# Differential attention: VectorE does all of the mix of the two softmaxes, GpSimd none

## The chip, the cores and the metric

The kernel runs on one core of a Trainium2 chip. The metric is the device time of one execution in microseconds (us), the median of the runs shown. One more execution was recorded by the hardware profiler; its page and its trace are what the prediction reads. Engines go by short names: PE (matmul; PEld is its weight load), DVE (VectorE), ACT (ScalarE), POOL (GpSimd), SP (the engine that issues most DMAs).

## The reference, cut to what matters

Two transformer layers over 2048 tokens of width 1024, float32. The first layer has three kinds of attention side by side; the change touches one, differential attention with six heads. Each head has two components with 32 features each; the weights of the second softmax, times lambda, are taken from those of the first, and the difference is multiplied with the values:

```python
s = jnp.einsum('bqhcd,bkhcd->bhcqk', qi, k) * scale
causal = key_idx[None, :] <= q_idx[:, None]
p = jax.nn.softmax(jnp.where(causal, s, NEG_BIG), axis=-1)
a = p[:, :, 0] - lam * p[:, :, 1]
return jnp.einsum('bhqk,bkhd->bqhd', a, v)
```

Afterwards comes an rms norm over the 64 features of each head. Since that norm takes out any factor common to a row, the kernel does not divide by the first softmax's sum s0. It forms exp0 + c * exp1 with c = -lambda * s0 / s1, one number for each row.

## The kernel before, in words

`differential` (line 599) handles 24 units in order: three pairs of heads p, two halves k, four steps j. A unit is two blocks of 128 queries, a high one and a low one, chosen so that their causal keys are 17 blocks of 128 together. The low block has nlo = 4k + j + 1 blocks of keys (1 to 8), the high one 17 - nlo (16 to 9). For each of the two heads and each of the two components a unit has one tile `row` of 2176 columns: first the high block's columns, then, from column n on, the low block's.

Three stages run one unit apart. While unit s + 2 has its scores computed, unit s + 1 is mixed and unit s is multiplied with the values.

- Scores (`diff_scores`): PE multiplies queries and keys into one of three PSUM banks `psz` (the tag "z": 3 in line 1386). DVE moves each chunk of up to 512 columns from there into `row`, times a scale, and keeps its smallest element in `mn` (line 725; line 727 where the causal mask applies; line 731 joins minima). ACT then takes the exponentials in place and sums them.
- Mix (`diff_mix`, line 748): DVE inverts the second sums (line 762) and forms the two factors c, one for each block of queries, in a tile `tiny` of 128x2 (line 766). Then exp0 + c * exp1 is formed over the 17 blocks. With a = 128 * max(0, 5 - nlo), GpSimd takes columns a to n in two instructions, a product in place (line 771) and a sum (line 772). DVE takes the low block's columns, n to 2176, in pieces of up to 1024, and columns 0 to a, each in one fused multiply-add `scalar_tensor_tensor` (line 778). So DVE takes max(5, nlo) of the 17 blocks, GpSimd the other 9 to 12.
- Values (`diff_values`): PE transposes blocks of `row` into PSUM (`pstp`), ACT copies them out (`wT`), PE multiplies with the values (`pspv`); after a chunk of queries comes the norm (`diff_norm`).

Between them go steps of `filler` (line 866), a share of the output projection: ACT and GpSimd split activations `mp` in two parts (line 901 is GpSimd's), PE multiplies them (`psmm`), DVE adds the residual (line 912). DVE itself splits five weight tiles `wo` (line 881).

PE's and ACT's instructions stay in the order in which the code writes them. DVE's, GpSimd's and SP's are put in an order by a scheduler when the kernel is built, and each engine works through its own in that order. In each unit the steps of scores and mix are spread over four beats; `diff_mix` returns its steps by beat, and the lists are mixed evenly with the work of the values and the filler.

Of the kernel before, what the change touches and what calls it, by code (L numbers as in the profile page):

```python
# [15 lines left out]
S = 2048  # L16
D = 1024
P = 128
# [16 lines left out]
VBLOCKS = 5  # L35
MIX = 1024
# [9 lines left out]
class Pinned:  # L46
    """An engine whose instructions stay in the order in which they are written."""
# [18 lines left out]
class Net:  # L66
# [16 lines left out]
    def phase(self, bufs, banks, side="left"):  # L83
        """Pools for one phase; SBUF slots and PSUM banks by tag."""
# [29 lines left out]
    def turn(self, key, pattern):  # L114
        """The next letter of a repeated pattern: which engine takes this one."""
        k = self.turns.get(key, 0)
        self.turns[key] = k + 1
        return pattern[k % len(pattern)]
# [8 lines left out]
    def consts(self):  # L127
# [5 lines left out]
        # nothing, then what is after the query (a column further on: at it or after it)  # L133
# [12 lines left out]
        # -lambda on every partition  # L146
# [26 lines left out]
    def rope_tables(self, k, sink):  # L173
        """cos and sin of the positions' angles, in chunks of 512: sink(chunk, cos, sin)."""
        nc = self.nc
        for t in range(NT):
# [5 lines left out]
            n = self.t("c2")  # L182
# [10 lines left out]
    def wtile(self, src):  # L193
        """A [P, 8, 128] tile of weights, as two parts."""
        w, (fill,) = self.wtile_steps(src, 1, self.nc.gpsimd)
        fill()
        return w
# [21 lines left out]
    def load_x(self, between):  # L219
        """x transposed, [tc][half] -> (hi, lo) of [P, 4, 512]."""  # L220
        nc = self.nc
        self.xs = []
        for t in range(NT):
            row = []
# [18 lines left out]
    def proj_t(self, w, t):  # L243
        """[128 features, 512 tokens] of chunk t."""
        return self.proj_side([w], t)[0]

    def proj_side(self, ws, t):
        """The same for several tiles of weights side by side."""
# [8 lines left out]
    def spill_parts(self, ps, dst, t, scale=None):  # L257
        """ps (times a power of two) in two parts to dst [2, P, S]."""
# [112 lines left out]
    def rope_all(self):  # L371
        """Both layers' tables to DRAM, a chunk of one at each next()."""
# [13 lines left out]
    def vtile(self, g):  # L386
        """Weights of 256 columns of the two attentions' values, as two parts of each half."""
# [9 lines left out]
    def values(self, g, ws, side):  # L397
        """256 columns of the two attentions' values, token by token."""
# [19 lines left out]
    def dup_parts(self, hi, lo, src, hh):  # L418
        """Half hh of src's partitions, its two parts in both halves of hi and lo."""
# [13 lines left out]
    def memkv(self, W, mem, keep):  # L433
        """Memory keys of each pair of heads and all values, a weight tile at each next()."""
# [35 lines left out]
    def tblocks(self, blocks, pattern="AV"):  # L470
        """Up to four [P, P] blocks transposed, in SBUF."""
# [8 lines left out]
    def softmax_pair(self, z, e, n0, sink=False):  # L480
        """z [P, 2, 256] -> e, normalised; columns from n0 on; the first is the sink's."""
# [13 lines left out]
    def mem_scores(self, qs, qcol, mk):  # L495
        """One block of queries, heads 2f and 2f+1 over the memory."""
# [20 lines left out]
    def load_qstack(self, src, t):  # L517
        """[P = two copies of 64, 2 heads, 2 parts, 512]."""
# [9 lines left out]
    def load_sb(self, p):  # L528
        """A pair of heads' keys and values and the last chunk's queries."""
# [69 lines left out]
    def differential(self):  # L599
        """Differential attention in three stages, each a unit (two blocks of queries, 17 blocks of  # L600
        keys together, of two heads) behind the one before: scores and exponentials; the mix of the
        two softmaxes; the product with the values. Between them go some feature tiles' share of
        the output projection."""
# [10 lines left out]
        def mixed(a, b):  # L614
            """Two lists evenly mixed, each in its order."""
# [58 lines left out]
    def load_dq(self, p, k, h):  # L674
        """Queries of a half of each of the two chunks: units j = 2h and 2h + 1."""
# [7 lines left out]
    def diff_parts(self, unit):  # L683
        """Of the two blocks of queries: their number, the chunk's, the place in it, the keys, the
        first column in a row."""
# [4 lines left out]
    def diff_scores(self, unit, rows):  # L690
        """For each head and component the steps of its scores, and those of the exponentials."""
# [56 lines left out]
    def diff_mix(self, unit, rows):  # L748
        """Steps by beat."""
        p, k, j = unit  # L750
        parts = self.diff_parts(unit)
        nlo = parts[1][3] // P
        a = P * max(0, VBLOCKS - nlo)
        cf = {}

        def take(steps):
            for f in steps:
                f()
# [9 lines left out]
        def mix(hh):  # L768
            x, y = rows[unit][0][2 * hh][0], rows[unit][0][2 * hh + 1][0]
            n = parts[0][3]  # L770
            self.nc.gpsimd.tensor_mul(y[:, a:n], y[:, a:n], cf[hh][:, :1].to_broadcast([P, n - a]))  # L771
            self.nc.gpsimd.tensor_add(x[:, a:n], x[:, a:n], y[:, a:n])  # L772
            pieces = [(c, min(c + MIX, 17 * P), 1) for c in range(n, 17 * P, MIX)]
            if a:
                pieces.append((0, a, 0))
            for lo, hi, w in pieces:
# [4 lines left out]

        late = [], []
        i0, f0, m0, l0 = lambda: inverse(0), lambda: factor(0), lambda: mix(0), lambda: take(late[0])
        i1, f1, m1, l1 = lambda: inverse(1), lambda: factor(1), lambda: mix(1), lambda: take(late[1])
        return [[i0, f0, m0], [l0, i1, f1, m1], [], [l1]]

# [35 lines left out]
    def diff_norm(self, p, t, s0, pv, tail):  # L822
        """rms norm over each head's 64, scaled by the first sum; the rest of its steps to tail."""
# [42 lines left out]
    def filler(self):  # L866
        """alpha x and the share of the output projection of the feature tiles known before the
# [608 lines left out]
```

## Time and profile before

| what | value |
|---|---|
| runs | 2661.22, 2660.3, 2658.35 us; median 2660.3 us |
| the profiled execution: its span, first to last instruction (no other time of it is shown) | 2665.1 us |
| busy in the span: PE, DVE, ACT, POOL | 2503.5, 1656.7, 1264.2, 1189.9 us |
| stretch from the first scores of differential attention to the last mix | 1115.7 to 1728.6 us, 612.9 us |

The span is 4.8 us longer than the median of the runs. A busy engine in a table of stretches is the union of its instructions. A PE row's time holds the passage through the array, so neighbouring PE rows overlap and a busy PE need not be at its fastest. PEclk is the share of its clock that PE was granted.

### The profile page before, as it was taken

How to read it: one execution, taken by the hardware profiler on the slowest of the kernel's cores; microseconds unless marked ns; L12 is line 12 of the kernel's file. 1: busy time of each engine (PE TensorE's matmuls, PEld its weight loads, DVE VectorE, ACT ScalarE, POOL GpSimd, SP SyncE). 2: the span in 40 equal slices, each digit the busy share in tenths (PEclk: the TensorE clock that was granted, in tenths of full speed). 3: DMA queues.
4: the chain of work that ended last, by engine and by line, in shares of the span. 5: the costliest groups of instructions: out<-in, count | busy, mean ns of one | idle time of the engine just before them, and what ended most of it. 6: DMA issues, size and time to landing. Idle time of an engine off the chain costs nothing. (4 is left out here: it accounts for less than half of the span.)

```text
span 2665.1 us, 42634 instructions
## 1 busy us (share of the span) xinstructions
PE 2503.5 (94%) x15564; PEld 1964.7 (74%) x15564; DVE 1656.7 (62%) x3672; ACT 1264.2 (47%) x2653; POOL 1189.9 (45%) x848
## 2 busy tenths in 40 slices
PE   9899999999989999968877988999999999999998
PEld 7788998888757777646655666678788777777887
DVE  5732223421379999888889878788321667677554
ACT  4532222221167777555665765744121677776200
POOL 1301004730056666465646746764541555535333
PEclk9999999999989999989988988999999999999999
DMA  7643223321842331442523422265332555532541
GB/s 273 212 146 125 70 88 105 137 103 52 203 104 70 82 71 34 99 116 73 127 78 95 108 76 74 70 215 173 88 101 75 162 154 162 152 96 99 194 147 67
DMA packets 199250, 311.60 MB, mean 117 GB/s; under 512 B 17921, under 2 KB 97281, under 8 KB 198529
## 3 DMA queue, kind: packets, MB, share of 16 engines
q1 hardware_dynamic: 198464, 307.83, 39.3%
q8 instruction: 123, 2.02, 0.3%
q10 hardware_dynamic: 576, 1.05, 0.1%
q14 instruction: 87, 0.70, 0.1%
HBM read 204.74 MB, written 104.07 MB: 116 GB/s over the span
## 5 line engine op out<-in xcount | busy, mean ns | idle before, releaser
L56 PE MATMUL psmm<-big,w 128*128 128x512 f32 x1680 | 415.4, 395 | 0.0
L56 PEld LDWEIGHTS psmm<-big,w 128*128 128x128 f32 x1680 | 306.8, 189 | 58.3
L586 POOL TENSOR_TENSOR wb<-wb,row 128x512 f32<-128x512 f32 (+3 forms) x192 | 219.5, 1154 | 136.4 <-DVE row L582 126.9
L582 DVE TENSOR_TENSOR_SCAN row<-psz,row,zero 128x512 f32<-128x512 f32 (+5 forms) x240 | 258.5, 1107 | 31.9 <-ACT psz L579 31.6
L253 PE MATMUL psmm<-big,w 128*128 128x512 f32 x1200 | 275.2, 389 | 0.0
L253 PEld LDWEIGHTS psmm<-big,w 128*128 128x128 f32 x1200 | 225.0, 188 | 47.0 <-issue 0.2
L56 ACT ACTIVATE row<-row,mn 128x2048 f32<-128x2048 f32 (+7 forms) x192 | 229.7, 1201 | 33.6 <-DVE mn L731 33.0
L56 PE MATMUL psmm<-big,mp 128*128 128x512 f32 x1056 | 244.5, 392 | 0.0
L725 DVE TENSOR_SCALAR_CACHE_REDUCE row<-psz 128x512 f32<-128x512 f32 (+1 forms) x324 | 200.9, 640 | 58.4 <-PE psz L56 55.9
L56 PEld LDWEIGHTS psmm<-big,mp 128*128 128x128 f32 x1056 | 198.3, 189 | 41.3 <-issue 0.3
L56 ACT COPY wT<-pstp 128x512 f32<-128x512 f32 (+3 forms) x240 | 121.4, 522 | 169.8 <-PE pstp L56 163.0
L1190 DVE TENSOR_TENSOR c<-psmm,c 128x512 f32<-128x512 f32 x62 | 42.6, 691 | 240.3 <-ACT c L1189 240.3
L592 PE MATMUL pspv<-wT,kv 128*64 128x128 f32 x1632 | 158.1, 287 | 15.4 <-ACT wT L122 15.4
L771 POOL TENSOR_TENSOR row<-row,tiny 128x1536 f32<-128x1536 f32 (+3 forms) x48 | 132.9, 2769 | 83.9 <-DVE tiny L766 78.1
L772 POOL TENSOR_TENSOR row<-row,row 128x1536 f32<-128x1536 f32 (+3 forms) x48 | 163.3, 3408 | 1.9
L208 POOL TENSOR_TENSOR w<-w,w 128x1024 fp32r<-128x1024 f32 x20 | 48.8, 2440 | 255.8 <-ACT w L207 155.4
L56 PE MATMUL psmm<-wo,mp 128*128 128x512 f32 x480 | 155.3, 437 | 3.1 <-ACT mp L56 2.3
L578 ACT ACTIVATE wb<-psz 128x512 f32<-128x512 f32 (+3 forms) x240 | 129.9, 541 | 53.6 <-PE pstp L475 37.2
L778 DVE SCALAR_TENSOR_TENSOR row<-row,tiny,row 128x128 f32<-128x128 f32 (+7 forms) x72 | 153.2, 2154 | 0.5
L573 PE MATMUL psz<-kv,qs 128*128 128x512 f32 (+3 forms) x480 | 150.0, 406 | 2.1 <-DVE row L582 2.0
L592 PEld LDWEIGHTS pspv<-wT,kv 128*64 128x64 f32 x1632 | 106.7, 139 | 60.5 <-issue 20.5
L56 PE MATMUL pstp<-ident,row 128*128 128x128 f32 x816 | 142.0, 297 | 9.7 <-DVE c L860 8.1
(222 smaller groups left out, 5241.6 us busy)
## 6 DMA issues: line engine op xcount, KB each, us to landing
silu<-c SPq DMA_DIRECT2D x54, 256.0 KB, 2.3
sl<-silu SPq DMA_DIRECT2D x54, 256.0 KB, 3.3
qs<-sbq SPq DMA_DIRECT2D x48, 256.0 KB, 5.3
cs<-rope SPq DMA_DIRECT2D x24, 512.0 KB, 4.4
kc<-k SPq DMA_DIRECT2D x36, 320.0 KB, 5.1
w<-in_we_dram SPq DMA_DIRECT2D x20, 512.0 KB, 3.7
raw<-in_wo_dram SPq DMA_DIRECT2D x20, 512.0 KB, 4.0
rx<-in_x_dram SPq DMA_DIRECT2D x32, 256.0 KB, 2.7
```

The costliest lines, as they stand in the source:

```text
L56: return self.tc.keep_in_program_order(f(*a, **k))
L208: eng.tensor_sub(lo[:, sl], raw[:, sl], hi[:, sl].bitcast(F32))
L253: self.nc.tensor.matmul(ps, w[a][:, c, :], self.xpart(t, c, b), start=(c == k == 0), stop=(c == 7 and k == 2))
L573: nc.tensor.matmul(z[:, :m], qs[:, hh, k, qcol], ks[hh][:, lo:hi], start=(k == 0), stop=(k == 1 and not diag))
L578: nc.scalar.activation(w[:, :m], z[:, :m], AF.Sigmoid, scale=0.125)
L582: nc.vector.tensor_tensor_scan(prr[:, lo + s0 - 1:hi - 1][:, ::-1], z[:, s0:m][:, ::-1], self.zero.to_broadcast([P, m - s0]), prr[:, hi - ...
L586: eng.tensor_mul(w[:, :m], w[:, :m], prr[:, lo:hi])
L592: nc.tensor.matmul(pv[64 * hh:64 * hh + 64, qcol], vp[:, blk, 64 * hh:64 * hh + 64], wT[hh][:, j * P:(j + 1) * P], start=(hi == n and j == ...
L725: nc.vector.tensor_scalar(e[:, col + lo:col + lo + n0], z[:, :n0], -scale, before, ALU.mult, ALU.min, accum_out=acc)
L771: self.nc.gpsimd.tensor_mul(y[:, a:n], y[:, a:n], cf[hh][:, :1].to_broadcast([P, n - a]))
L772: self.nc.gpsimd.tensor_add(x[:, a:n], x[:, a:n], y[:, a:n])
L778: self.nc.vector.scalar_tensor_tensor(x[:, lo:hi], y[:, lo:hi], cf[hh][:, w:w + 1], x[:, lo:hi], ALU.mult, ALU.add)
```

## The change

Lines 771 and 772 go. `scalar_tensor_tensor` on DVE now covers all 2176 columns of each head in three pieces: the low block's columns, and the high block's in two halves. The pieces are placed over the beats: two of the first head in beat 0, its third in beat 1; the second head's in beats 1, 2 and 3. The constants VBLOCKS and MIX go. Elsewhere the diff only blanks docstrings and comments, so code lines move up by two, and by eight to thirteen in and behind `diff_mix`.

```diff
-        nlo = parts[1][3] // P
-        a = P * max(0, VBLOCKS - nlo)
...
         def mix(hh):
             x, y = rows[unit][0][2 * hh][0], rows[unit][0][2 * hh + 1][0]
             n = parts[0][3]
-            self.nc.gpsimd.tensor_mul(y[:, a:n], y[:, a:n], cf[hh][:, :1].to_broadcast([P, n - a]))
-            self.nc.gpsimd.tensor_add(x[:, a:n], x[:, a:n], y[:, a:n])
-            pieces = [(c, min(c + MIX, 17 * P), 1) for c in range(n, 17 * P, MIX)]
-            if a:
-                pieces.append((0, a, 0))
-            for lo, hi, w in pieces:
+            for w, (lo, hi) in ((1, (n, 17 * P)), (0, (0, n // 2)), (0, (n // 2, n))):
                 def piece(lo=lo, hi=hi, w=w):
                     self.nc.vector.scalar_tensor_tensor(x[:, lo:hi], y[:, lo:hi], cf[hh][:, w:w + 1], x[:, lo:hi], ALU.mult, ALU.add)
                 late[hh].append(piece)
             late[hh].pop(0)()
+        def take(hh, k):
+            for f in late[hh][:k]:
+                f()
+            del late[hh][:k]
...
-        return [[i0, f0, m0], [l0, i1, f1, m1], [], [l1]]
+        return [[i0, f0, m0, lambda: take(0, 1)], [lambda: take(0, 1), i1, f1, m1], [lambda: take(1, 1)], [lambda: take(1, 1)]]
```

What stands on DVE around one head's mix early in a pair of heads (first pair, nlo = 2; the number behind a name is the tile's own). Before:

```order
L762 RECIPROCAL tiny_11077<-tiny_10885 128x2
L731 TENSOR_REDUCE mn_10976<-mn_10976 128x1
L766 SCALAR_TENSOR_TENSOR tiny_11077<-s_1986_10724,nlam,tiny_11077 128x2
L778 SCALAR_TENSOR_TENSOR row_10886<-row_10928,tiny_11077,row_10886 128x256
L778 SCALAR_TENSOR_TENSOR row_10886<-row_10928,tiny_11077,row_10886 128x384
L725 TENSOR_SCALAR row_11013,mn_11014<-psz_11015 128x512
L725 TENSOR_SCALAR row_11013,mn_11014<-psz_11019 128x512
```

The same place on DVE now (lines 758, 765 and 723 are the former 766, 778 and 725):

```order
L758 SCALAR_TENSOR_TENSOR tiny_11075<-s_1986_10724,nlam,tiny_11075 128x2
L765 SCALAR_TENSOR_TENSOR row_10886<-row_10927,tiny_11075,row_10886 128x256
L765 SCALAR_TENSOR_TENSOR row_10886<-row_10927,tiny_11075,row_10886 128x960
L723 TENSOR_SCALAR row_11011,mn_11012<-psz_11013 128x512
L765 SCALAR_TENSOR_TENSOR row_10886<-row_10927,tiny_11075,row_10886 128x960
L723 TENSOR_SCALAR row_11011,mn_11012<-psz_11017 128x512
```

DVE had 640 columns of this head between two reads of scores and has 2176 now, with one read of scores ahead of the last piece.

Late in a pair of heads (nlo = 8), on DVE before:

```order
L766 SCALAR_TENSOR_TENSOR tiny_12585<-s_2201_11536,nlam,tiny_12585 128x2
L727 ISA row_12466,mn_12467<-psz_12489,mask 128x128
L727 ISA mn_12467 128x1
L778 SCALAR_TENSOR_TENSOR row_12275<-row_12356,tiny_12585,row_12275 128x1024
L731 TENSOR_REDUCE mn_12467<-mn_12467 128x1
L725 TENSOR_SCALAR row_12466,mn_12467<-psz_12497 128x512
```

And now:

```order
L758 SCALAR_TENSOR_TENSOR tiny_12577<-s_2201_11530,nlam,tiny_12577 128x2
L723 TENSOR_SCALAR row_12457,mn_12458<-psz_12459 128x512
L723 TENSOR_SCALAR row_12457,mn_12458<-psz_12466 128x512
L765 SCALAR_TENSOR_TENSOR row_12267<-row_12347,tiny_12577,row_12267 128x1024
L765 SCALAR_TENSOR_TENSOR row_12267<-row_12347,tiny_12577,row_12267 128x576 x2
L725 ISA row_12457,mn_12458<-psz_12481,mask 128x128
```

Here DVE had 1024 columns and has 2176, the three pieces in one run.

On GpSimd at the end of the first five units, before:

```order
L901 TENSOR_TENSOR mp_11701<-mp_11639,mp_11700 128x640
L771 TENSOR_TENSOR row_11616<-row_11616,tiny_11800 128x1536
L772 TENSOR_TENSOR row_11548<-row_11548,row_11616 128x1536
L771 TENSOR_TENSOR row_11729<-row_11729,tiny_11878 128x1536
L772 TENSOR_TENSOR row_11678<-row_11678,row_11729 128x1536
L901 TENSOR_TENSOR mp_11881<-mp_11810,mp_11880 128x640
L849 TENSOR_TENSOR tiny_12010<-tiny_12010,mhalf 128x8
```

And now (line 893 is the former 901, line 841 the former 849):

```order
L893 TENSOR_TENSOR mp_11689<-mp_11632,mp_11688 128x640
L893 TENSOR_TENSOR mp_11873<-mp_11803,mp_11872 128x640
L841 TENSOR_TENSOR tiny_12002<-tiny_12002,mhalf 128x8
L843 TENSOR_TENSOR c_2305_11952<-c_2305_11952,tiny_12002 128x512
```

Every product and sum of the mix is gone from GpSimd; the splits of the filler and the steps of the norm stay. PE and ACT have the same instructions, a few transposes and products of the values a few places earlier or later.

More of the change, by code (lines that the diff above doesn't have):

```diff
@@ L34 @@
 GATES_A = 3
-VBLOCKS = 5
-MIX = 1024
 HEAD = 2
@@ L751, in diff_mix @@
         parts = self.diff_parts(unit)
-        nlo = parts[1][3] // P
-        a = P * max(0, VBLOCKS - nlo)
         cf = {}
-        def take(steps):
-            for f in steps:
-                f()
         def inverse(hh):
@@ L780, in mix @@
             late[hh].pop(0)()
+        def take(hh, k):
+            for f in late[hh][:k]:
+                f()
+            del late[hh][:k]
         late = [], []
-        i0, f0, m0, l0 = lambda: inverse(0), lambda: factor(0), lambda: mix(0), lambda: take(late[0])
-        i1, f1, m1, l1 = lambda: inverse(1), lambda: factor(1), lambda: mix(1), lambda: take(late[1])
-        return [[i0, f0, m0], [l0, i1, f1, m1], [], [l1]]
+        i0, f0, m0 = lambda: inverse(0), lambda: factor(0), lambda: mix(0)
+        i1, f1, m1 = lambda: inverse(1), lambda: factor(1), lambda: mix(1)
+        return [[i0, f0, m0, lambda: take(0, 1)], [lambda: take(0, 1), i1, f1, m1], [lambda: take(1, 1)], [lambda: take(1, 1)]]
     def diff_values(self, unit, rows, tail):
```

## The prediction

> **What bounds the kernel now.** I read the page's groups first, then stretches of the part that the change touches, then who waits for whom in it, then single instructions in order of time. The columns of a group are: line, engine, operation, tiles, shape, count | busy us, mean ns of one | idle time of the engine before them.
>
> ```profile
> span 2665.1 us, 42634 instructions
> L771 POOL TENSOR_TENSOR row<-row,tiny 128x1536 f32<-128x1536 f32 (+3 forms) x48 | 132.9, 2769 | 83.9 <-DVE tiny L766 78.1
> L772 POOL TENSOR_TENSOR row<-row,row 128x1536 f32<-128x1536 f32 (+3 forms) x48 | 163.3, 3408 | 1.9
> L778 DVE SCALAR_TENSOR_TENSOR row<-row,tiny,row 128x128 f32<-128x128 f32 (+7 forms) x72 | 153.2, 2154 | 0.5
> ```
>
> The first thing to see is the mean of line 778. Its 72 instructions cover 46 blocks for one head of each of the eight units (5 + 5 + 5 + 5 + 5 + 6 + 7 + 8), times 2 heads and 3 pairs: 276 blocks or 35,328 columns, 491 each. That is 4.4 ns for a column. By shape:
>
> ```profile
> L778 DVE SCALAR_TENSOR_TENSOR row<-row,tiny,row 128x128 f32<-128x128 f32 x12 | 26.5, 2208 | 0.0
> L778 DVE SCALAR_TENSOR_TENSOR row<-row,tiny,row 128x512 f32<-128x512 f32 x12 | 33.4, 2780 | 0.0
> L778 DVE SCALAR_TENSOR_TENSOR row<-row,tiny,row 128x1024 f32<-128x1024 f32 x6 | 12.2, 2038 | 0.1
> L778 DVE SCALAR_TENSOR_TENSOR row<-row,tiny,row 128x768 f32<-128x768 f32 x6 | 9.2, 1531 | 0.0
> L778 DVE SCALAR_TENSOR_TENSOR row<-row,tiny,row 128x896 f32<-128x896 f32 x6 | 8.0, 1341 | 0.1
> ...
> L778 DVE SCALAR_TENSOR_TENSOR row<-row,tiny,row x72: 341/2304/3993, 1135.4 to 1724.0; 128x128 f32<-128x128 f32 x12, 128x512 f32<-128x512 f32 x12, 128x256 f32<-128x256 f32 x12, 128x384 f32<-128x384 f32 x12
> ```
>
> 128 columns take as long as 1024, and the shortest instruction (341 ns; the last row gives min/median/max) is a sixth of the mean. So most of this time is no work of DVE. A timeline (start, length, engine, instruction) shows what it is:
>
> ```profile
> 1217.07 2.75 POOL L771 TENSOR_TENSOR row<-row,tiny 128x1536 f32<-128x1536 f32 x1
> 1217.12 6.67 DVE L778 SCALAR_TENSOR_TENSOR row<-row,tiny,row 128x512 f32<-128x512 f32 x2
> 1219.90 3.74 POOL L772 TENSOR_TENSOR row<-row,row 128x1536 f32<-128x1536 f32 x1
> 1223.71 0.14 DVE L731 TENSOR_REDUCE mn<-mn 128x1 f32<-128x4 f32 x1
> 1224.87 0.47 PE L56 MATMUL psz<-kc,qa 128*128 128x512 f32 x1 [4.10 <-DVE mn L727]
> ```
>
> Two pieces start beside line 771 and end at 1223.79, as line 772 does at 1223.64: DVE stands until GpSimd is done. Nothing reads the three banks `psz` meanwhile, so PE stops for 4.10 us before its next score product. How much of the stage goes this way:
>
> ```profile
> PE psz L56 <- DVE row L725: 43.2, 27, 9.1
> PE psz L56 <- DVE mn L727: 35.7, 16, 4.9
> ...
> DVE row L725 <- PE psz L56: 59.3, 72, 3.9
> DVE row L727 <- PE psz L56: 24.0, 29, 2.4
> ...
> PEld pstp L56 <- POOL row L771: 2.0, 2, 1.0
> ```
>
> The columns are who <- for whom, us in total, times, longest. PE waits 78.9 us in 43 waits for DVE to read scores; DVE waits 83.3 us for PE to write them, much of it after PE has been stopped. The stretches (length, busy time of PE, PEld, DVE, ACT, POOL with counts, PE's clock, DMA share, GB/s), first the stage, then three early parts (nlo 1 to 5), then three late parts (nlo 6 to 8):
>
> ```profile
> 1115.70:1728.60 612.90, 511.12 (x3334) 363.60 (x3334) 507.89 (x1397) 379.02 (x677) 371.08 (x147) 0.90 0.36 94
> 1134.80:1278.10 143.30, 112.61 (x663) 79.71 (x662) 120.44 (x303) 80.89 (x145) 79.20 (x30) 0.87 0.36 96
> 1338.50:1484.00 145.50, 112.18 (x761) 80.11 (x760) 126.16 (x312) 87.22 (x158) 78.58 (x30) 0.87 0.32 85
> 1543.50:1681.30 137.80, 118.08 (x766) 83.89 (x766) 111.25 (x304) 85.05 (x154) 80.95 (x31) 0.88 0.25 69
> 1278.10:1338.50 60.40, 53.48 (x372) 37.84 (x370) 49.36 (x153) 40.06 (x72) 44.48 (x20) 0.94 0.56 131
> 1484.00:1543.50 59.50, 54.41 (x388) 38.83 (x388) 49.08 (x161) 42.78 (x78) 44.64 (x20) 0.97 0.44 110
> 1681.30:1728.60 47.30, 44.42 (x337) 31.82 (x337) 38.87 (x117) 34.18 (x63) 40.12 (x18) 1.00 0.20 59
> ```
>
> DVE is busy for 507.9 of 612.9 us (83%) and **DVE bounds the stage**: in the early parts PE stands idle or at a clock of 0.87 while DVE waits. In the late parts, where DVE's pieces seldom stand, PE gets through more: the weight loads (PEld), a fixed amount of work, are busy for 243.7 of 426.6 us early (57%) and 108.5 of 167.2 us late (65%).
>
> **The change, part by part.**
>
> ```profile
> L1029 DVE SCALAR_TENSOR_TENSOR rx<-rx,tiny,gb x32: 744/750/754, 2497.6 to 2661.5; 128x512 f32<-128x512 f32 x32
> L1026 DVE SCALAR_TENSOR_TENSOR rx<-rx,tiny,gb x32: 1262/1284/1992, 1748.7 to 2658.7; 128x1024 f32<-128x1024 f32 x32
> L766 DVE SCALAR_TENSOR_TENSOR tiny<-s,nlam,tiny x48: 207/221/2549, 1134.5 to 1723.8; 128x2 f32<-128x2 f32 x48
> L881 DVE TENSOR_TENSOR wo<-rx,wo x5: 677/690/3168, 1394.9 to 1433.2; 128x512 fp32r<-128x512 f32 x5
> ...
> L766 DVE SCALAR_TENSOR_TENSOR tiny<-s,nlam,tiny 128x2 f32<-128x2 f32 x48 | 26.1, 543 | 0.5
> L881 DVE TENSOR_TENSOR wo<-rx,wo 128x512 fp32r<-128x512 f32 x5 | 8.2, 1635 | 0.0
> ...
> L901 POOL TENSOR_TENSOR mp<-mp,mp x32: 1532/1565/2387, 1057.0 to 1709.8; 128x640 fp32r<-128x640 f32 x32
> ```
>
> 1. The fused multiply-adds. Lines 1026 and 1029 are the same operation on tiles in SBUF, little disturbed. Their medians give (1284 - 750) / 512 = 1.043 ns a column and 750 - 534 = 216 ns an instruction. For 128 columns that makes 350 ns, and line 778's own shortest is 341, so the line holds for these tiles. Now there are 3 x 48 = 144 pieces over 48 x 17 x 128 = 104,448 columns: 108.9 + 31.1 = **140.0 us in place of 153.2**. Three times the columns cost DVE 13.2 us less. The price's own spread (1262 against 1284) is 2%, 3 us.
> 2. Line 766, a 128x2 instruction, has a mean of 543 ns and a median of 221: 26.1 - 48 x 0.221 = 15.5 us of standing go. Line 881 likewise: 8.2 - 5 x 0.690 = 4.7 us.
> 3. GpSimd's 132.9 + 163.3 = 296.2 us go. Only 2.0 us of waiting was for them, so as such they are worth nothing; but line 901 no longer queues behind 6 us of mix.
> 4. What is left on GpSimd still meets DVE: some 30 splits of line 901 at 1.57 us in the stage. The bounds are 0 and 30 x 1.57 = 47 us of DVE. A burst of pieces comes every 11.7 us (560 / 48), so a split starts just ahead of one in some 1.57 / 11.7 = 13% of cases and holds it for half its length: 30 x 0.13 x 0.8 = 3 us. I take 3, as these splits stood there before, too.
> 5. Places. A head's pieces are now a run of about 2.9 us (2176 x 1.043 + 3 x 0.216), partly with a read of scores between. The shapes of 768, 896 and 1024 columns are those of late heads: 9.2 + 8.0 + 12.2 = 29.4 us in 18 heads, 1.6 us each. The other 153.2 - 29.4 = 123.8 us are those of 30 early heads, 4.1 us each. So early runs shorten by 1.2 us and late ones grow by 1.3. Behind a run queue the reads of `psz`, then PE. PE writes some 20 chunks of scores in a unit (five for each of four rows), and a unit takes about 560 / 24 = 23 us; three banks then cover 3 / 20 of that, 3.5 us by this estimate. A run of 2.9 us is just covered, one of 4.1 or 6.67 us isn't. The transposes read a row only a unit later, so the pieces that moved to later beats make nobody wait.
>
> Sum for DVE: 507.9 - 13.2 - 15.5 - 4.7 + 3 = 477.5 us. At the share of today (0.829) the stage takes 576 us, 37 less. The other end is PE's pace: at the late parts' share of weight loads the 363.6 us would take 363.6 / 0.649 = 560 us, at that of the last part (31.82 / 47.30 = 0.673) 540 us, 73 less. DVE would then be busy for 85 and 88%. Shorter runs and a higher clock should remove some of the idle time, but late heads get more work than they had, so I take 563 us, between the ends: **50 us less**. The rest of the kernel has the same instructions and is taken at nothing. The span is 4.8 us longer than the median, which no term of this needs; I take the 50 us from the median: 2660.3 - 50 = **2610 us**.
>
> The Trainium skill, "VectorE: DVE Perf Modes", section on the trn2 errata, gives (N + 151) / 0.96 ns for a float32 `tensor_tensor`; an estimate by it is (104,448 + 144 x 151) / 0.96, 131 us. The rows of the fused form lie above that (1284 ns for 1024 columns against 1224 by the page), and the sum goes by the rows.
>
> **The rivals.**
>
> ```profile
> PE psz L56 <- DVE mn L727: 0.8, 2, 0.5
> ...
> PE psz L56 <- DVE row L725: 0.6, 2, 0.4
> ```
>
> These are PE's waits for reads of scores in the first late part (1278.1 to 1338.5 us).
>
> - PE's pace decides. If three banks cover every run and the clock stays up, the stage goes as its last part does now: 540 us, 2587 in all. For it: a clock of 1.00 in the last part, and in the first late part PE waited 1.4 us for DVE in all. Against: DVE would have to be busy for 88%, and has not been above 87% (126.16 of 145.50) in any part. The Trainium skill, "TensorE: Matmul & The Clock Gate", Part 1, says that the clock halves after an idle window of about 3.4 us; the 0.87 beside waits of 4 to 9 us agrees, and with runs of 2.9 us no such halving would be left.
> - GpSimd's remaining work takes the place of the mix. If half of line 901's time falls on DVE's runs, which are now twice as many instructions, DVE gets 24 us back, 28 in the stage: 2638. For it: line 1026's longest is 1992 ns. Against: 30 splits stand against 96 long instructions today. The Trainium skill, "SBUF — State Buffer", section "Who interferes with whom", calls it a lock held for a whole instruction by whoever started first; by it a run of DVE makes the split wait as often.
> - Slower: the early units' pace is not set by line 778's standing, and the late ones pay. Then 18 heads x 1.3 us = 23 us, 28 at DVE's share, come on top: 2688. It decides if early parts keep above 28 us a unit (426.6 / 15) although no piece stands. Against it: PE's 78.9 us of waits for DVE.
> - That the change doesn't do what it says: its order has no mix on GpSimd, so no.
>
> **How the numbers follow.** The forecast has 0.53, PE's pace 0.23, the small gain 0.13, slower 0.06; 0.05 is left for a gain that another wait takes whole. About 0.2% (5 us) can be told from no change. Faster 0.53 + 0.23 + 0.13 = 0.89, same 0.05, slower 0.06. The range goes from 2580, just past PE's pace, to 2645, past the small gain; it leaves out the two worst cases and the tails.
>
> **What would show it.** The fused multiply-adds: 144 with a busy time near 140 us, 1024 columns near 1.3 us. The factor's instruction near 0.22 us. DVE some 478 us busy in a stage of about 563. PE's waits for reads of scores well under 78.9 us, none of 9 us, its clock above 0.90. Early units nearer to 23 us than 28. It is wrong if the pieces still take 2 us for 128 columns, if PE's waits stay with short pieces, or if time appears after the stage.

## The result and the profile after

The changed kernel takes **2599.82 us** (median of 4 runs, 2597.49 to 2603.45) against 2659.96 us for the kernel before beside it (4 runs, 2658.35 to 2661.22). The ratio is 0.9778, with a 95% interval of 0.9764 to 0.9791: 60 us less, where 50 were predicted, and inside the range.

The page of the changed kernel, its groups (columns as before; lines 765, 758 and 873 are the former 778, 766 and 881):

```profile
span 2601.7 us, 42463 instructions
...
L765 DVE SCALAR_TENSOR_TENSOR row<-row,tiny,row 128x128 f32<-128x128 f32 (+7 forms) x144 | 142.1, 1037 | 0.5
L758 DVE SCALAR_TENSOR_TENSOR tiny<-s,nlam,tiny 128x2 f32<-128x2 f32 x48 | 13.7, 286 | 0.4
L873 DVE TENSOR_TENSOR wo<-rx,wo 128x512 fp32r<-128x512 f32 x5 | 3.4, 689 | 0.0
L765 DVE SCALAR_TENSOR_TENSOR row<-row,tiny,row 128x1024 f32<-128x1024 f32 x18 | 23.5, 1334 | 0.1
L765 DVE SCALAR_TENSOR_TENSOR row<-row,tiny,row 128x128 f32<-128x128 f32 x6 | 2.1, 347 | 0.1
```

Three times the columns take 142.1 us where a third of them took 153.2. The 128-column form went from 2208 to 347 ns, the 1024-column form from 2038 to 1334: the time now goes with the columns.

The stretches of the changed kernel (length, busy PE, PEld, DVE, ACT, POOL, PE's clock, DMA share, GB/s): the stage, the three early parts (nlo 1 to 5), the three late parts (nlo 6 to 8):

```profile
1117.30:1663.20 545.90, 484.08 (x3332) 343.13 (x3334) 478.23 (x1470) 378.37 (x677) 86.71 (x51) 0.96 0.41 105
1136.70:1252.20 115.50, 99.50 (x658) 69.91 (x656) 100.15 (x312) 79.03 (x141) 15.32 (x9) 0.96 0.44 115
1315.90:1430.20 114.30, 99.92 (x750) 71.30 (x750) 103.61 (x321) 85.44 (x156) 14.34 (x10) 1.00 0.39 105
1496.70:1610.40 113.70, 105.10 (x755) 74.70 (x754) 100.82 (x314) 83.34 (x152) 18.38 (x12) 0.98 0.30 84
1252.20:1315.90 63.70, 55.48 (x377) 39.31 (x375) 56.43 (x169) 41.50 (x78) 12.89 (x8) 0.95 0.55 132
1430.20:1496.70 66.50, 60.25 (x399) 42.55 (x400) 58.70 (x177) 44.12 (x80) 12.71 (x8) 0.90 0.41 103
1610.40:1663.20 52.80, 47.80 (x345) 34.08 (x345) 45.78 (x131) 36.11 (x66) 9.95 (x6) 0.97 0.16 48
```

| | before | after | difference |
|---|---|---|---|
| early parts, 15 units | 426.6 us, 28.4 a unit | 343.5 us, 22.9 a unit | -83.1 us |
| late parts, 9 units | 167.2 us, 18.6 a unit | 183.0 us, 20.3 a unit | +15.8 us |
| stage | 612.9 us, DVE busy 507.9 (83%) | 545.9 us, DVE busy 478.2 (88%) | -67.0 us |
| rest of the span | 2052.2 us | 2055.8 us | +3.6 us |

So the gain has two signs in it: the early units, where GpSimd had 12 blocks, win 83 us, and the late ones, where DVE had 6 to 8 blocks itself and got 9 to 11 on top, are 16 us longer; DVE is busy for 160.9 us in them, where it was for 137.3. The profiled execution of the changed kernel is the longest of its four runs (2603.45 us), and the span of the one before is 4.8 us above that kernel's median, so differences between the two traces are good to a few us.

Who waits for whom in the stage of the changed kernel (who <- for whom: us, times, longest):

```profile
DVE row L723 <- PE psz L54: 37.0, 67, 3.1
PE psz L54 <- DVE row L723: 28.8, 34, 2.6
PE psz L54 <- DVE mn L725: 12.2, 14, 2.0
DVE row L725 <- PE psz L54: 8.7, 23, 1.0
```

PE's waits for reads of scores went from 78.9 us in 43 to 41.0 us in 48, the longest from 9.1 to 2.6 us; DVE's waits for PE from 83.3 to 45.7 us. One place shows both sides of the collision. Timelines of the same point of the program (second head of the first unit), before and then after:

```profile
1146.09 3.46 POOL L772 TENSOR_TENSOR row<-row,row 128x1536 f32<-128x1536 f32 x1
...
1147.98 1.59 DVE L766 SCALAR_TENSOR_TENSOR tiny<-s,nlam,tiny 128x2 f32<-128x2 f32 x1
```

```profile
1150.30 0.21 DVE L758 SCALAR_TENSOR_TENSOR tiny<-s,nlam,tiny 128x2 f32<-128x2 f32 x1
1150.55 2.75 DVE L765 SCALAR_TENSOR_TENSOR row<-row,tiny,row 128x128 f32<-128x128 f32 x3
1152.45 2.28 POOL L893 TENSOR_TENSOR mp<-mp,mp 128x640 fp32r<-128x640 f32 x1 [4.00 <-ACT mp L54]
```

Before, the factor of two columns lasts 1.59 us and ends at 1149.57, with GpSimd's sum at 1149.55. After, it lasts 0.21 us, a head's run of three pieces 2.75 us, and now it is GpSimd that stands: its split takes 2.28 us where its median is 1.57, 0.71 us longer, and 0.85 us of the run were left when it began (1153.30 - 1152.45).

### The profile page after: what moved, and what is told of

Same layout as the page of the kernel before. It is cut to its first block, busy times and chain, and to the rows that moved or that the text cites. A ratio compares the mean times of both kernels' runs of the same rounds, so it can differ in the third digit from the quotient of the medians.

```text
span 2601.7 us, 42463 instructions
## 1 busy us (share of the span) xinstructions
PE 2475.1 (95%) x15564; PEld 1943.0 (75%) x15564; DVE 1628.2 (63%) x3744; ACT 1264.3 (49%) x2653; POOL 907.8 (35%) x752
## 5 line engine op out<-in xcount | busy, mean ns | idle before, releaser
L893 POOL TENSOR_TENSOR mp<-mp,mp 128x640 fp32r<-128x640 f32 x32 | 57.0, 1781 | 341.4 <-ACT mp L54 280.7
L590 PEld LDWEIGHTS pspv<-wT,kv 128*64 128x64 f32 x1632 | 106.1, 138 | 63.7 <-issue 20.3
L54 PE MATMUL psmm<-wo,mp 128*128 128x512 f32 x480 | 149.7, 423 | 3.9 <-ACT mp L54 3.0
L765 DVE SCALAR_TENSOR_TENSOR row<-row,tiny,row 128x128 f32<-128x128 f32 (+7 forms) x144 | 142.1, 1037 | 0.5
L1181 ACT ACTIVATE c<-psmm 128x512 f32<-128x512 f32 x62 | 36.7, 596 | 211.8 <-PE psmm L251 203.9
L473 PE MATMUL pstp<-ident,wb 128*128 128x128 f32 x816 | 135.2, 285 | 0.0
```

What stands on the lines that cost most here:

```text
L54: return self.tc.keep_in_program_order(f(*a, **k))
L473: self.nc.tensor.transpose(ps[:, j * P:(j + 1) * P], b, self.ident)
L590: nc.tensor.matmul(pv[64 * hh:64 * hh + 64, qcol], vp[:, blk, 64 * hh:64 * hh + 64], wT[hh][:, j * P:(j + 1) * P], start=(hi == n and j == ...
L765: self.nc.vector.scalar_tensor_tensor(x[:, lo:hi], y[:, lo:hi], cf[hh][:, w:w + 1], x[:, lo:hi], ALU.mult, ALU.add)
L893: self.nc.gpsimd.tensor_sub(ml, m, mh.bitcast(F32))
```

## The experiments

Twelve kernels ran. The table gives the time, and the stretch from the first product of scores to the last product with the values, which all of them have, with DVE and GpSimd busy in it and PE's clock. Beside them the kernel before gave 2651.47 us (one run, for the first four), 2658.4 us (7 runs, the next four), 2660.23 us (7, the two after) and 2657.65 us (7, the last two).

| kernel | us | stretch | DVE | POOL | clock |
|---|---|---|---|---|---|
| before | 2659.96 | 627.0 | 513.5 | 377.7 | 0.90 |
| after | 2599.82 | 559.9 | 484.0 | 90.3 | 0.96 |
| reads | 2678.58 | 636.6 | 545.1 | 369.2 | 0.90 |
| writes | 2596.20 | 556.2 | 481.5 | 397.1 | 0.97 |
| nomix | 2546.57 | 505.2 | 401.7 | 80.9 | 0.99 |
| two_banks | 2674.86 | 636.3 | 503.3 | 86.4 | 0.92 |
| code_order | 2591.94 | 550.2 | 480.8 | 83.0 | 0.98 |
| gpsimd_all | 2606.05 | 566.2 | 414.4 | 507.2 | 0.94 |
| gpsimd_all_factor | 2596.03 | 554.0 | 387.2 | 506.9 | 0.95 |
| split_11 | 2648.42 | 606.6 | 511.3 | 270.5 | 0.93 |
| gpsimd_scalar_mul | 2700.93 | 657.8 | 392.0 | 600.7 | 0.88 |
| gpsimd_order | 2779.65 | 737.7 | 393.5 | 597.9 | 0.84 |
| scalar_half | 2588.59 | 549.2 | 380.6 | 407.7 | 0.95 |
| scalar_all | 2632.16 | 591.9 | 380.7 | 313.7 | 0.93 |

code_order and the last four are medians of 4 runs; the other eight experiments are one run each. What lies ahead of the stretch (1113.1 to 1117.4 us) and behind it (921.7 to 925.3 us) differs by no more than that between all fourteen profiled executions, though the code there is the same; the changed kernel's is the longest ahead and the second longest behind. So its +3.6 us outside the stage lie within what these places scatter. A stretch is that of the one profiled execution of its kernel.

### Is it GpSimd's reading, or its being busy?

**reads**: to the changed kernel GpSimd's product and sum are given back, at their former sizes, on the second component's row after the last piece has used it, where nothing needs the outcome.

```diff
         def take(hh, k):
...
             del late[hh][:k]
+            if late[hh]:
+                return
+            x, y = rows[unit][0][2 * hh][0], rows[unit][0][2 * hh + 1][0]
+            n = parts[0][3]
+            a = P * max(0, 5 - parts[1][3] // P)
+            self.nc.gpsimd.tensor_mul(y[:, a:n], y[:, a:n], cf[hh][:, :1].to_broadcast([P, n - a]))
+            self.nc.gpsimd.tensor_add(y[:, a:n], y[:, a:n], x[:, a:n])
```

> The changed kernel, with GpSimd work put back that computes nothing needed: after the last piece of a head's mix, a product and a sum of the former size (1152 to 1536 columns) on the second row, which nobody reads any more. The result stays that of the reference. Theory (a piece of DVE that reads two tiles stands while a GpSimd instruction reads): the pieces go from 142 us to 190 to 260 us, the stage from 546 to 590 to 650, the time to 2640 to 2710 us. Rival (GpSimd's mix was only late or in line 901's way): pieces stay at 142 us, time 2600 within 8.

**writes**: five fills in place of the two last lines.

```diff
-            self.nc.gpsimd.tensor_mul(y[:, a:n], y[:, a:n], cf[hh][:, :1].to_broadcast([P, n - a]))
-            self.nc.gpsimd.tensor_add(y[:, a:n], y[:, a:n], x[:, a:n])
+            for _ in range(5):
+                self.nc.gpsimd.memset(y[:, a:n], 0.0)
```

> The same places, but GpSimd only writes: five memsets of the same columns of that row in place of product and sum, so that it is busy about as long. The result stays that of the reference. Theory (it is GpSimd's reading that makes DVE stand): pieces 142 us within 8, time 2600 within 8. Rival (any GpSimd work on SBUF makes DVE stand): pieces 190 to 260 us, time 2640 to 2710 us, as with reads.

Groups of the stretch of reads, then of writes:

```profile
L765 DVE SCALAR_TENSOR_TENSOR row<-row,tiny,row 128x128 f32<-128x128 f32 (+7 forms) x144 | 169.7, 1226 | 0.5
L779 POOL TENSOR_TENSOR row<-row,row 128x1536 f32<-128x1536 f32 (+3 forms) x48 | 157.9, 3290 | 3.5
L778 POOL TENSOR_TENSOR row<-row,tiny 128x1536 f32<-128x1536 f32 (+3 forms) x48 | 124.5, 2593 | 114.7 <-DVE row L765 107.4 <-DVE mn L729 6.5 <-DVE tiny L754 0.8
L758 DVE SCALAR_TENSOR_TENSOR tiny<-s,nlam,tiny 128x2 f32<-128x2 f32 x48 | 43.4, 903 | 0.4
L911 DVE SCALAR_TENSOR_TENSOR rx<-rx,psmm 128x512 f32<-128x512 f32 x32 | 21.8, 682 | 4.5 <-PE psmm L54 4.3
```

```profile
L779 POOL MEMSET row<- 128x1536 f32 (+3 forms) x240 | 310.5, 1300 | 57.8 <-DVE row L765 45.1 <-DVE mn L729 2.9
L765 DVE SCALAR_TENSOR_TENSOR row<-row,tiny,row 128x128 f32<-128x128 f32 (+7 forms) x144 | 140.5, 1025 | 0.5
L758 DVE SCALAR_TENSOR_TENSOR tiny<-s,nlam,tiny 128x2 f32<-128x2 f32 x48 | 13.5, 282 | 0.4
L911 DVE SCALAR_TENSOR_TENSOR rx<-rx,psmm 128x512 f32<-128x512 f32 x32 | 21.9, 683 | 3.0 <-PE psmm L54 2.9
```

310.5 us of fills cost nothing that shows: pieces, factor and stretch are as in the changed kernel, and the time is 3.6 us below its median (one run, beside which the kernel before was itself 8.5 us below its median). 282.4 us of products and sums (157.9 + 124.5) make it 82.4 us longer than with the fills, on the same chip: pieces +29.2, factor +29.9, stretch +80.4. PE's waits for reads of scores are 89.6 us in reads and 40.5 in writes: what stands on DVE stops PE. The time and the stretch came as on record for the theory; the pieces took 169.7 us, less than the 190 to 260 on record, and the factor took the other half of the standing. Line 911 (the residual) is the same operation with one tile in SBUF and one in PSUM: 682 ns in reads and 683 in writes, so it doesn't stand. What holds DVE is GpSimd's reading of SBUF beside a DVE instruction with two tiles there, not GpSimd's being busy. The Trainium skill, "SBUF — State Buffer", section "Who interferes with whom", says that a DVE instruction with two SBUF inputs contends with a GpSimd instruction that reads SBUF and not with one that only writes; the pair of runs agrees.

### What does the mix still cost DVE?

**nomix**: the kernel before without GpSimd's share of the mix; DVE keeps its 72 pieces.

```diff
-            self.nc.gpsimd.tensor_mul(y[:, a:n], y[:, a:n], cf[hh][:, :1].to_broadcast([P, n - a]))
-            self.nc.gpsimd.tensor_add(x[:, a:n], x[:, a:n], y[:, a:n])
```

> The kernel before without lines 771 and 772: GpSimd's 9 to 12 blocks of the mix of each head are left out, DVE's own pieces stay. It shows the stage with neither the standing nor the work that the change adds to DVE. Theory: the 72 pieces take 48 us in place of 153 and the factors 11 in place of 26, DVE is busy some 385 us; if DVE's work still bounds the changed kernel (478 of 546 us), the stage is shorter than there, 500 to 530 us, and the time 2555 to 2585. Rival (PE's pace bounds the changed kernel's stage already): 540 to 546 us, time 2595 to 2600.

```profile
L776 DVE SCALAR_TENSOR_TENSOR row<-row,tiny,row 128x128 f32<-128x128 f32 (+7 forms) x72 | 51.2, 738 | 0.5
L766 DVE SCALAR_TENSOR_TENSOR tiny<-s,nlam,tiny 128x2 f32<-128x2 f32 x48 | 17.7, 368 | 0.5
```

These groups of nomix show the same 72 pieces with nothing beside them: 51.2 us where before they took 153.2. The stretch is 121.8 us shorter than before, and the time 104.9 us below that of the kernel before beside it (2651.47 - 2546.57), below the 2555 to 2585 us on record; that is all that GpSimd's 9 to 12 blocks cost there. The change gets 67.1 us of the stretch back. The other 54.7 us go with DVE's new work, 82.3 us more busy time than in nomix (484.0 - 401.7), so DVE still bounds the changed kernel's stage. Moving the work was worth it only since the standing that it caused on DVE had cost still more.

### Do three banks cover the run?

**two_banks**: the changed kernel with two banks of `psz` (the third goes to the transposes).

```diff
-                            {"mm": 1, "z": 3, "tp": 2, "pv": 2}):
+                            {"mm": 1, "z": 2, "tp": 3, "pv": 2}):
```

> The changed kernel with two banks for scores in place of three (the bank goes to the transposes). Theory of step 5 (three banks just cover a run of 2.74 us, so PE hardly stops): with two a run isn't covered, PE's waits for reads of scores rise from 41 us by 0.8 us a run or more, to 80 to 130 us, time 2630 to 2690 us. Rival (only DVE's sum of work counts): waits within 10 us of 41, time 2600 within 8.

**code_order**: the changed kernel with DVE's instructions in differential attention kept in the order of the code, which puts reads of scores between most pieces.

```diff
-        self.nc = PinnedCore(nc, self.tc, ("tensor", "scalar"))
+        self.nc = PinnedCore(nc, self.tc, ("tensor", "scalar", "vector"))
```

> The changed kernel with DVE's instructions, too, kept in the order of the code through differential attention. The same work, but a head's three pieces no longer stand in one run of 2.74 us: nearly always a read of scores stands between them. Theory of step 5 (a run that the banks just cover still costs a little): PE's waits for reads of scores go from 41 us to 15 to 30 us, time 2565 to 2595 us. Rival (the runs cost nothing; a fixed order makes DVE wait for exponentials that the scheduler went around): DVE's waits for ACT go from 13 us to 30 us or more, time 2600 to 2650 us.

PE's waits for reads of scores, two_banks first, then code_order (where DVE's instructions carry the helper's line):

```profile
PE psz L54 <- DVE row L723: 62.7, 51, 3.8
PE psz L54 <- DVE mn L725: 30.3, 20, 3.3
```

```profile
PE psz L54 <- DVE mn L54: 16.1, 23, 1.8
PE psz L54 <- DVE row L54: 12.2, 29, 2.0
```

With two banks PE waits 93.0 us, more than before the change, and the whole gain is gone although the pieces take 143.4 us as a group: a run of 2.75 us is longer than two banks cover. With three it waits 41.0 us, and with three banks and shorter runs 28.3. code_order takes 2591.94 us (2589.98 to 2593.9; ratio 0.9754, 0.9738 to 0.9770). All its runs lie below all of the changed kernel's, by 8 us in the median; by the ratios, each against the kernel before beside it, it is some 6 us, and their intervals just touch (0.9770 and 0.9764). The cover by the banks is thus a condition of the gain, and by PE's waits not full with three.

### Other divisions of the same work

**gpsimd_all**: the opposite division. GpSimd takes all 17 blocks, DVE none.

```diff
-        a = P * max(0, VBLOCKS - nlo)
+        a = 0
...
-            pieces = [(c, min(c + MIX, 17 * P), 1) for c in range(n, 17 * P, MIX)]
...
-            late[hh].pop(0)()
+            self.nc.gpsimd.tensor_mul(y[:, n:], y[:, n:], cf[hh][:, 1:].to_broadcast([P, 17 * P - n]))
+            self.nc.gpsimd.tensor_add(x[:, n:], x[:, n:], y[:, n:])
```

> The other end: GpSimd does the whole mix, product and sum over all 17 blocks, DVE none of it (lines 766 and 762 stay on DVE). Theory: DVE's work falls by the pieces' 142 us, but line 766, which reads two tiles, stands behind GpSimd, 48 times up to 4 us, 60 to 150 us in all; GpSimd is busy some 450 us with the mix (104,448 columns at 1.9 and 2.4 ns). Stage 540 to 620 us, time 2590 to 2675 us. Rival (GpSimd's share is only bad through DVE's pieces): line 766 at its 0.22 us, the stage near nomix's, time 2545 to 2580 us.

**gpsimd_all_factor**: the same, with the factor in two instructions of 128x1 that have one tile and two numbers per partition, in place of one with two tiles.

```diff
-            self.nc.vector.scalar_tensor_tensor(cf[hh], self.dsum[p, k][:, i0:i1 + 1:i1 - i0], self.nlam, cf[hh], ALU.mult, ALU.mult)
+            for w, i in enumerate((i0, i1)):
+                self.nc.vector.tensor_scalar(cf[hh][:, w:w + 1], self.dsum[p, k][:, i:i + 1], self.nlam, cf[hh][:, w:w + 1], ALU.mult, ALU.mult)
```

> As gpsimd_all, with line 766 written as two instructions that read one tile and two columns of scalars each. Theory (only an instruction with two tiles to read stands): they take 0.2 us each and don't stand, time 20 to 90 us below gpsimd_all, 2555 to 2620 us, where GpSimd's 450 us of mix and 50 of splits bound the stage at 520 to 560 us. Rival (any reading of DVE stands behind GpSimd): no change against gpsimd_all within 8 us.

**split_11**: the kernel before with a division in the middle, 11 blocks on DVE and 6 on GpSimd.

```diff
-VBLOCKS = 5
+VBLOCKS = 11
```

> The kernel before with VBLOCKS at 11 in place of 5: DVE takes 11 of 17 blocks, GpSimd 6, two thirds of the blocks moved that the change moves. Theory (standing goes with GpSimd's time): GpSimd's mix 155 to 165 us, pieces and factors of DVE 130 to 175 us, time between the two kernels, 2615 to 2645 us. Rival (a share for GpSimd takes work from DVE and a middle is best): below 2595 us.

The factor in gpsimd_all as a group and as one line's instructions (min/median/max in ns), and the same in gpsimd_all_factor behind GpSimd's two products; then the three groups of the mix in split_11:

```profile
L766 DVE SCALAR_TENSOR_TENSOR tiny<-s,nlam,tiny 128x2 f32<-128x2 f32 x48 | 57.0, 1188 | 0.7
L766 DVE SCALAR_TENSOR_TENSOR tiny<-s,nlam,tiny x48: 207/664/6268, 1134.7 to 1658.0; 128x2 f32<-128x2 f32 x48
```

```profile
L772 POOL TENSOR_TENSOR row<-row,tiny 128x2048 f32<-128x2048 f32 (+7 forms) x48 | 137.2, 2858 | 9.5 <-DVE tiny L767 8.2 <-ACT wT L56 0.8 <-PE psmm L56 0.5
L774 POOL TENSOR_TENSOR row<-row,tiny 128x128 f32<-128x128 f32 (+7 forms) x48 | 55.7, 1161 | 0.0
L767 DVE TENSOR_SCALAR tiny<-s,nlam,tiny 128x1 f32<-128x1 f32 x96 | 22.0, 267 | 0.7
L767 DVE TENSOR_SCALAR tiny<-s,nlam,tiny x96: 256/266/275, 1135.7 to 1646.1; 128x1 f32<-128x1 f32 x96
```

```profile
L778 DVE SCALAR_TENSOR_TENSOR row<-row,tiny,row 128x128 f32<-128x128 f32 (+7 forms) x96 | 163.2, 1739 | 0.5
L772 POOL TENSOR_TENSOR row<-row,row 128x768 f32<-128x768 f32 x48 | 101.4, 2115 | 2.7
L771 POOL TENSOR_TENSOR row<-row,tiny 128x768 f32<-128x768 f32 x48 | 81.9, 1706 | 113.5 <-DVE tiny L766 101.9 <-ACT wT L56 11.0
```

In gpsimd_all a multiplication of two columns takes up to 6.27 us and 57.0 us in all, just under the 60 to 150 on record. With one tile read it never stands (256 to 275 ns), beside the same 436 us of mix on GpSimd. The run is 10 us shorter, one run against one on the same chip, and less than the 20 to 90 on record: the factor's standing is shown by its rows, but it cost the kernel little; GpSimd is busy for some 90% of the stretch in both runs. Both ends of the division are thus good: 2599.82 us with all on DVE, 2596.03 with all on GpSimd and no two-tile factor. The middle isn't between them: split_11 takes 2648.42 us, above the 2615 to 2645 on record for it. By the price of point 1 of the prediction its 48 x 11 x 128 = 67,584 columns in 96 pieces are 91 us of work (70.5 + 20.7); they take 163.2. GpSimd's mix fell by 38% (296.2 to 183.3 us), but DVE's standing only from 101 us (153.2 - 52.4 by the same price) to 72, while DVE's own work grew by 39. More pieces meet less GpSimd work, and both are paid.

### Is there a version that beats both?

In gpsimd_all_factor GpSimd is busy for 506.9 of 554.0 us (91%), DVE for 387.2. So GpSimd's work was to be made shorter, in three ways.

**gpsimd_scalar_mul**: the product as a multiplication by one number per partition, and one sum a head.

```diff
-            self.nc.gpsimd.tensor_mul(y[:, a:n], y[:, a:n], cf[hh][:, :1].to_broadcast([P, n - a]))
-            self.nc.gpsimd.tensor_add(x[:, a:n], x[:, a:n], y[:, a:n])
-            self.nc.gpsimd.tensor_mul(y[:, n:], y[:, n:], cf[hh][:, 1:].to_broadcast([P, 17 * P - n]))
-            self.nc.gpsimd.tensor_add(x[:, n:], x[:, n:], y[:, n:])
+            for w, (lo, hi) in enumerate(((0, n), (n, 17 * P))):
+                self.nc.gpsimd.tensor_scalar_mul(y[:, lo:hi], y[:, lo:hi], cf[hh][:, w:w + 1])
+            self.nc.gpsimd.tensor_add(x[:, :17 * P], x[:, :17 * P], y[:, :17 * P])
```

> As gpsimd_all_factor (all of the mix on GpSimd, the factor in two 128x1 instructions of one tile), but GpSimd's product is written as a multiplication by one number per partition (one tile read) and the sum is one instruction per head over all 17 blocks. The question is whether GpSimd was the bound there (506.9 us busy of 554.0) and what the product costs. If a product of one tile runs nearer to the pace of the fills (310.5 us for 240, 1.3 us for 1,536 columns, 0.85 ns a column), the 192.7 us of products come to some 90, GpSimd is busy for about 405 us, its bound is gone and the stretch goes from 554 towards the 505 of nomix: 2555 to 2580 in all. If it costs as much as before (1.85 ns a column), the time stays within 5 us of 2596. Should it cost more, GpSimd bounds harder and the time rises above 2600. In each case the factor stays near 22 us for 96, since it has one tile.

**gpsimd_order**: the same, with DVE in the order of the code (the edit of code_order).

```diff
-        self.nc = PinnedCore(nc, self.tc, ("tensor", "scalar"))
+        self.nc = PinnedCore(nc, self.tc, ("tensor", "scalar", "vector"))
```

> As gpsimd_scalar_mul, with DVE's instructions kept in the order of the code in the differential attention, as in code_order. Theory: the gain of code_order (8 us) came from shorter runs of pieces between DVE's reads of scores; here DVE has no pieces, so the order is worth nothing: within 4 us of gpsimd_scalar_mul. Rival: the order helps by itself (reads of scores ahead of other work on DVE), then it gives some 8 us here too.

Two groups of gpsimd_scalar_mul, a wait of it, and three waits of gpsimd_order:

```profile
L773 POOL TENSOR_SCALAR row<-row,tiny 128x2048 f32<-128x2048 f32 (+7 forms) x96 | 290.8, 3043 | 12.1 <-DVE tiny L767 11.7
L774 POOL TENSOR_TENSOR row<-row,row 128x2176 f32<-128x2176 f32 x48 | 232.2, 4848 | 0.6
```

```profile
PE pstp L56 <- POOL row L774: 120.5, 20, 14.6
```

```profile
DVE row L56 <- PE psz L56: 299.9, 200, 14.5
...
PE pstp L56 <- POOL row L774: 174.0, 43, 9.6
POOL row L773 <- DVE tiny L56: 100.9, 28, 10.4
```

The third case came: one number per partition makes GpSimd's product dearer, 290.8 us for 104,448 columns or 2.8 ns each, where the product with a broadcast factor took 192.9 us in gpsimd_all_factor (137.2 + 55.7), 1.85 ns. Against that run GpSimd's busy time rose by 93.8 us and the stretch by 103.8, and its share stayed at 91%: GpSimd bounds this form, and PE waits for its sums before the transposes. gpsimd_order missed both expectations. DVE has no pieces to part there; its order by the code puts the factor behind reads of scores that wait for PE (299.9 us), GpSimd waits 100.9 us for the factor, PE 174.0 us for GpSimd. So the order is no gain by itself. That agrees with a gain of code_order through its pieces, but doesn't show it, since here the order also moved the factor.

**scalar_half**: gpsimd_all_factor, with head 0's products on ScalarE a beat later; GpSimd has head 1's products and both sums, each sum in one instruction (these lines aren't shown).

```diff
+            if hh == 0:
+                def prod():
+                    for w, (lo, hi) in enumerate(((0, n), (n, 17 * P))):
+                        self.nc.scalar.mul(y[:, lo:hi], y[:, lo:hi], cf[hh][:, w:w + 1])
+                    self.nc.gpsimd.tensor_add(x[:, :17 * P], x[:, :17 * P], y[:, :17 * P])
+                late[hh].append(prod)
+                return
...
```

> As gpsimd_all_factor (no mix on DVE, the factor in 128x1 instructions), but head 0's products go to ScalarE a beat later; GpSimd keeps head 1's products and both sums. gpsimd_scalar_mul made GpSimd's work 87 us longer (435.9 to 523.0) and the whole 105 us slower, so GpSimd sets the pace there. Theory: that holds in the other direction: GpSimd loses 96 us of products (436 to 340, with the splits some 411 busy), ScalarE gains 52,224 columns at 0.84 ns and 48 times 0.28 us, 57 us, and is at about 436 of 520. The bound passes back to PE and DVE, the stretch goes from 554 to 515-530: 2560 to 2575 in all. Rival: ScalarE's copies of transposes to wT queue behind the products, which wait for the factor; then PE waits for pstp, and the gain is lost: 2590 or more.

**scalar_all**: both heads' products on ScalarE, head 1's in the third beat.

```diff
-            if hh == 0:
+            if True:
...
-        return [[i0, f0, m0], [l0, i1, f1, m1], [], [l1]]
+        return [[i0, f0, m0], [l0, i1, f1, m1], [l1], []]
```

> As scalar_half, with both heads' products on ScalarE (head 1's in the third beat); GpSimd has the sums alone. GpSimd has 243 us of mix, some 315 busy; ScalarE gains 115 us and is at about 494. If ScalarE's queue stays harmless, the time is within 10 us of scalar_half or better, 2555 to 2575, and no lower than nomix's 2547. If ScalarE becomes the bound (busy for over 90% of the stretch, as GpSimd was in gpsimd_all_factor at 506.9 of 554.0), it gives 494 / 0.92 = 537 us: about 2580, slower than scalar_half.

The group of the products on ScalarE in scalar_half, PE's two largest sums of waits there, and two waits of scalar_all:

```profile
L56 ACT ACTIVATE row<-row,tiny 128x2048 f32<-128x2048 f32 (+15 forms) x48 | 55.2, 1200 | 0.0
```

```profile
PE pstp L56 <- POOL row L781: 24.3, 7, 6.6
PE pstp L56 <- ACT c L56: 5.6, 7, 1.7
```

```profile
POOL row L776 <- ACT row L56: 176.8, 37, 11.9
PE pstp L56 <- POOL row L776: 42.0, 19, 4.5
```

scalar_half takes **2588.59 us** (2586.12 to 2590.18; ratio 0.9734, 0.9715 to 0.9753), the fastest of those that compute the whole. Its interval lies below the changed kernel's; with code_order's it overlaps. The products cost ScalarE 55.2 us, as expected (57), and GpSimd is busy for 74% of the stretch; yet the time is near that of the rival (2590 or more) and not the 2560 to 2575 of the theory, by a wait that neither theory had named: the transposes of head 1 wait for its sum, 24.3 us. ScalarE, GpSimd and DVE all have room there (78, 74 and 69% busy); the likely reading, which no run takes apart, is that the way from the exponentials over factor, product and sum to the transposes has become too long. In scalar_all each sum waits for ScalarE, which has exponentials and products in the order of the code: 176.8 us of waiting on GpSimd and 42.0 on PE. It takes 2632.16 us, above both times on record for it (2555 to 2575, and 2580). The second of these had ScalarE busy for over 90% of the stretch; it is busy for 82%, so the time goes with these waits and not with a full engine.

## Why the prediction was right

1. **The fused multiply-adds** were to take 140.0 us: 142.1 in the changed kernel, 140.5 in writes. The price by column and instruction from other lines held.
2. **The factor and the weights' split**: 10.6 and 3.45 us forecast, 13.7 and 3.4 measured (the longest factor took 1275 ns).
3. **GpSimd's 296 us are worth nothing as such**: 310.5 us of fills on it cost nothing that shows.
4. **Collisions with what is left on GpSimd**: 3 us taken of 0 to 47. Pieces and factor are 2.1 and 3.1 us above their prices, 5.2 us. The splits stand as well, as the timeline shows, and PE waited 0.4 us for a split in the whole stage, its weight loads 1.6 us. The rival of GpSimd's remaining work (2638 us) falls with it.
5. **Places**: a run of 2.9 us just covered by three banks. Most runs of three pieces take about 2.75 us, a few up to 4.06; PE's waits for reads of scores fell to 41.0 us and none is over 2.6. two_banks shows that the cover is needed, code_order that it leaves something.
6. **The sum** of 477.5 us for DVE: 478.2. The signs hold: 22.9 us a unit early, a clock of 0.96. Only the aside that no halving of PE's clock would be left does not hold: in the second late part the clock is 0.52 from 1436 to 1440 us and 0.57 from 1480 to 1484 us, although PE's longest wait there is 2.8 us.

The mis-sized term is the last one, from DVE's busy time to the length of the stage: 563 us were taken, 545.9 came. With 477.5 us of DVE that meant a share of 85%, and 88% came out. Two steps of the prediction leaned too low. First, it held against PE's pace that DVE "has not been above 87%" in any part; but those parts were the ones in which DVE stood and PE was stopped by it. In the changed kernel it is busy for 91% of an early part (103.61 of 114.30). Second, the end at PE's pace, 540 us, took the weight loads' 363.6 us as a fixed amount of time. It fell with the higher clock, to 343.1 us at 0.96, and nomix runs the whole stretch, which is longer than the stage, in 505.2 us. So 540 us were no floor: the result went three quarters of the way from the forecast's 563 to it, for DVE still bounds the stage.

The slower rival was a real effect with too small a place. Late parts did pay, 15.8 us where it priced 23 to 28; but it could decide only if the early ones had kept above 28 us a unit, and they fell to 22.9. So the distance between the forecast's 50 us and the 67 in the stage lies in this step alone. In the span it is 63.4 us (2665.1 - 2601.7), and in the medians 60; what the span has less than the stage is scatter outside it.

## What to carry to other kernels

If an instruction's time doesn't go with its columns, price the work by its shortest instances or by the same operation elsewhere: work can be cheaper on a busier engine when sharing it with another makes that engine stand. Where DVE and GpSimd read SBUF beside each other, look at both ends of a division before the middle, and write small DVE instructions with one tile. After such a move, check the buffers in front of the lengthened run, and take the new length of the stage from a share that the engine reaches where it isn't stopped.

## What the runs showed of the hardware

- GpSimd's product by one number per partition took 2.8 ns a column and its product with a broadcast factor 1.85 ns, its sum 2.2 (4848 ns for 2176 columns), and its fill 0.9 ns (1380 ns for 1536 columns).
- A DVE instruction of 128x2 elements with two tiles stood for up to 6.27 us beside GpSimd; one of 128x1 with a tile and two numbers per partition never took more than 275 ns.
- GpSimd's fills, 310.5 us of them, neither slowed DVE's two-tile instructions (1025 ns a piece against 1037) nor the kernel.
